# A hybrid encoder step on one core: a weight block's six matmuls become five, and each unit's two partial sums are added by ACT and DVE

## The chip, the cores and the metric

The kernel runs on one core of a Trainium2 chip. The metric is the time of one execution on the device in microseconds (us). Engine names are those of the profile: PE is TensorE's matmul (PEld its weight load), DVE is VectorE, ACT is ScalarE, POOL is GpSimd, SP is SyncE, whose queue (SPq) issues the DMAs.

## The reference

Two layers of an encoder step over 544 tokens (512 of a prompt, 32 of a second request) with 1024 features. Everything is float32.

```python
u = x @ w_in                      # 1024 -> 8192, split into qa ka va za qb kb vb zb xr zc ga gb gc
ya = band_attention(qa, ka, va, rel_table)          * silu(za)
yb = group_norm(retention(rope(qb), rope(kb), vb))  * silu(zb)
yc = rg_lru(conv(xr))                               * silu(zc)
m  = sigmoid(ga) * (ya @ w_branch[0]) + sigmoid(gb) * (yb @ w_branch[1]) + sigmoid(gc) * (yc @ w_branch[2])
r  = ALPHA * x + m @ w_out
r  = r + sigmoid(r @ w_ple_gate) * (p[l] @ w_ple)
x  = layer_norm(r)                # input of the next layer
```

The outputs are x after the second layer, and the caches and states of both layers.

## The kernel before

**Layout.** Activations lie with features on the 128 partitions and the N = 544 tokens along the free dimension. A float32 product is made of three products in the type fp32r: each operand is split into a high part (rounded to fp32r) and a low part (what is left), and high x high, high x low and low x high are summed in PSUM. `hilo` (L254) makes the two parts of an activation, a copy on ACT and a subtraction on DVE; `split` (L198) does the same for two blocks of weights at a time, 128x256 values.

**Blocks and units.** The weights come from memory in chunks of 8 blocks of 128x128 (tile `raw`, 512 KB, four buffers). A *unit* is 128 output features: a tile of PSUM named `mm` takes the sums of 2 blocks (kind `pl`, the per-layer embedding), 4 blocks (`bA`, `bB`, `bC`, the branch products) or 8 blocks (all others). `layer_units` (L33) lists the units of a layer in order: 8 `pl`; 4 `xr`, of which the first two form one group that fills both `mm` tiles block by block; `va`, `qa`/`ka` in turns, `kb`, `vb`, `qb`; then for each branch four `z` units and eight times a `g` unit and a `b` unit; then 8 `wo` and 8 `pg`.

`block` (L237) issues a block's six matmuls: for each of (weights high, x high), (weights high, x low), (weights low, x high), one for each half of the tokens, 272 columns each. A tile `mm` is two banks of PSUM of 512 float32; each half of the tokens has a bank of its own. There are two such tiles, so PE can fill one while the other is emptied by `evac` (L788): by ACT, by DVE or by both, according to the kind of the unit.

**Order.** The order of the work is written out by hand. Each engine executes its instructions in the order in which the program issues them. Before each block `tick` (L165) is called: it lets `stream` (L208) issue the splits up to `LEAD` = 8 blocks ahead, and it advances the *jobs*: generators for attention, retention, the recurrence (rg_lru) and the layer norm, which issue a few instructions and then sleep for the number of ticks that they yield (table `PACE`). So the side work is woven in between the blocks. Split weights lie in seven buffers of two blocks each (pool `wp`, tiles `wh` and `wl`), or in `held` tiles of a chunk where they are kept longer.

**Ends of a layer.** The last `pg` units (from the 7th in layer 0, from the 3rd in layer 1, `HELD`) and the first two `xr` units of layer 1 are computed by halves of the tokens (`by_halves`, L932): first all blocks of half 0, then those of half 1, so that the layer norm of half 0 (`ln_job`, L730) runs beside the matmuls of half 1. In layer 1's beginning the `pl` units run while the layer norm of layer 0 is under way. At the start of the kernel `x_job` (L994) makes the parts of the eight input tiles, one every two ticks from tick 5 on, beside the `pl` units of layer 0.

**Storage of the parts.** The high and low parts of x are in four slabs: two for the high parts (`xh`), two for the low ones (`xl`), four feature tiles each. The same holds for the gated branch outputs (`zah`, `zal` and so on), for m (`mh`, `ml`) and, in one slab, for the embedding (`phl`).

Of the kernel before, what the change touches and what calls it, by code (L numbers as in the profile page):

```python
# [19 lines left out]
H2 = N // 2  # L20
PAST = 256
# [96 lines left out]
def encoder(ctx: ExitStack, tc, xT, pT, W, RB, KC, VC, PAR, CST, o_y, o_k, o_v, o_rp, o_rs, o_cv, o_lr):  # L118
# [7 lines left out]
    wp = pool("wp", LEAD // 2 + 3)  # L126
# [71 lines left out]
    def split(n, h, lo):  # L198
        t = raw[n // 8][:, n % 8:n % 8 + 2]
        S.copy(h, t)  # L200
        V.tensor_tensor(lo, t, h.bitcast(F32), SUB)  # L201
        parts[n // 2] = (h, lo)

    def hold(n):
        held[n // 8] = sl("held", F32R, (128, 2, 8, 128))
        return [[held[n // 8][:, i, k:k + 2] for i in range(2)] for k in range(0, 8, 2)]

    def stream(lead=LEAD):  # L208
        while at["split"] < L * NB and at["split"] <= at["use"] + at["more"] + lead:
            n = at["split"]  # L210
            kind, f, k = BLOCKS[n % NB]
            if n // 2 not in parts:
                if kind == "wg" or kind == "pg" and f >= HELD[n // NB]:
                    if n % 8 == 0:
                        at["hold"] = hold(n)
                    h, lo = at["hold"][n % 8 // 2]
                else:
                    h = wp.tile([128, 2, 128], F32R, tag="wh", name="wh")
                    lo = wp.tile([128, 2, 128], F32R, tag="wl", name="wl")
                split(n, h, lo)  # L220
                if n % 8 == 6:
                    load()
            at["split"] += 2


    def split_ahead(l):
        for c in range((l + 1) * NCH, (l + 1) * NCH + (AT["xr"] + 16) // 8):
            t = wr.tile([128, 8, 128], F32, tag="raw", name="raw")
            raw[c] = t
            Q.dma_start(out=t, in_=W[c // NCH, c % NCH])  # L230
            views = hold(8 * c)
            yield 8
            for i, v in enumerate(views):
                split(8 * c + 2 * i, *v)
                yield 3

    def block(ps, xh, xl, first, last, hfs=(0, 1), n=None):  # L237
        if n is None:
            n = at["use"]
            at["use"] += 1  # L240
        h, lo = parts[n // 2]
        for i, (w, x) in enumerate(((h, xh), (h, xl), (lo, xh))):
            for hf in hfs:
                T.matmul(ps[:, hf, :H2], lhsT=w[:, n % 2, :], rhs=x[:, hf * H2:(hf + 1) * H2],  # L244
                         start=first and i == 0, stop=last and i == 2)

    def halves(ap):
        return ap.rearrange("p (a b) -> p a b", a=2)
# [10 lines left out]
    def busy(n):  # L259
        ps = psum("mm")  # L260
        for _ in range(n):
            T.matmul(ps[:, 0, :H2], lhsT=zero[:, :128], rhs=zero, start=True, stop=True)  # L262


    st = {"xh": [sl("xh", F32R) for _ in range(2)], "xl": [sl("xl", F32R) for _ in range(2)]}
# [3 lines left out]
    def ple_load(l):  # L269
        pr = sl("pr")  # L270
        ple_in[l] = (pr, sl("phl", F32R))
        for k in range(2):
            Q.dma_start(out=pr[:, k], in_=pT[l, :, k])

    def ple_split(l):
        pr, p2 = ple_in[l]
        for k in range(2):
            hilo(p2[:, k], p2[:, 2 + k], pr[:, k])
# [34 lines left out]
    def layer(l, env, nxt):  # L313
# [165 lines left out]
        def lru_tile(t):  # L479
# [12 lines left out]
            for g in range(2):  # L492
                w, lo = ([parts[(l * NB + AT["wg"] + g * 4 + t) // 2][i][:, t % 2] for i in range(2)])
# [206 lines left out]
        def span(hf):  # L700
            return slice(0, N) if hf is None else slice(hf * H2, (hf + 1) * H2)

# [6 lines left out]
        def ln_center():  # L709
            yield PACE["center"]  # L710
            c, s2 = tmp("center"), env["s2p"]
            for h in range(2):
                ps = psum("sc")
                T.matmul(ps[:, :H2], lhsT=cst[:, C_O1K:C_O1K + 128], rhs=env["acc"][:, span(h)])
                S.mul(c[:, span(h)], ps[:, :H2], 4.0)
# [11 lines left out]
        PIECES = [(c if i < 2 else H2 - 128, c, min(128, H2 - c), 0 if i < 2 else 128 - (H2 - c))  # L727
                  for i, c in enumerate((0, 128, 256))]

        def ln_job(hf):  # L730
            ones = cst[:, C_O1K:C_O1K + 1]
            if hf and l == L - 1:
                busy(WARM[1])
            ps = psum("tp")
            for q, src in enumerate((env["s1"], env["s2"])):
                for i, (c0, _, _, _) in enumerate(PIECES):
                    T.matmul(ps[:, 3 * q + i:3 * q + i + 1], lhsT=src[:, hf * H2 + c0:hf * H2 + c0 + 128], rhs=ones)
# [3 lines left out]
            mu, e2, sq, A, B = (w[:, 3 * i:3 * i + 3] for i in range(5))  # L741
            V.tensor_copy(w[:, 0:6], ps[:, 0:6])
            V.tensor_tensor(sq, mu, mu, MUL)
            V.scalar_tensor_tensor(sq, e2, EPS, sq, ADD, SUB)
            G.tensor_tensor(A, sq, mhalf, ALU.pow)
# [3 lines left out]
            for q, src in enumerate((B, A)):  # L749
                ps = psum("sc" if hf == 0 else "tp" if q == 0 else "pv")  # L750
                for i, (_, d0, n, i0) in enumerate(PIECES):
                    T.matmul(ps[:, d0:d0 + n], lhsT=bc(src[:, i:i + 1], [[0, 128]]), rhs=ident[:, i0:i0 + n])
                AB.append(ps[:, :H2])
# [9 lines left out]
            for f in range(9):  # L763
# [11 lines left out]
                if f and not last:  # L775
                    e = f - 1
                    h, lo = (st[k][e // 4][:, e % 4, span(hf)] for k in ("xh", "xl"))
# [10 lines left out]
        def evac(kind, t, ps, hf=None):  # L788
            pv = ps[:, :, :H2]
            if kind in KEY:  # L790
# [3 lines left out]
                d = halves(env[key][:, t])  # L794
# [4 lines left out]
                if kind == "ka":  # L799
# [3 lines left out]
                    V.tensor_copy(env["kn"][:, t], ps[:, 1, H2 - NS:H2])  # L803
# [13 lines left out]
            elif kind == "qa":  # L817
# [3 lines left out]
                h = halves(env["QTh"][:, t])  # L821
                S.mul(h, pv, 0.125)
                V.scalar_tensor_tensor(halves(env["QTl"][:, t]), pv, 0.125, h.bitcast(F32), MUL, SUB)
                S.mul(env["qs"][:, t], ps[:, 1, H2 - NS:H2], 0.125)
            elif kind == "xr":
# [5 lines left out]
                S.copy(xrp[:, t, 3:3 + H2], ps[:, 0, :H2])  # L831
                S.copy(xrp[:, t, 3 + H2:3 + NP], ps[:, 1, :NP - H2])
                S.copy(xrp[:, t, NP + 6:], ps[:, 1, NP - H2:H2])  # L833
# [4 lines left out]
            elif kind in ("za", "zb", "zc"):  # L838
# [15 lines left out]
            elif kind[0] == "g":
                sg = tmp("sg")
                S.activation(halves(sg), pv, AF.Sigmoid)  # L856
                env["sg", t] = sg
            elif kind[0] == "b":
                sg = env.pop(("sg", t))
                a, b = t // 4, t % 4  # L860
                if kind == "bC":
                    if b == 0:
                        env["m", a] = sl("m")
                    V.tensor_tensor(halves(env["m", a][:, b]), pv, halves(sg), MUL)
                else:
                    V.tensor_tensor(halves(sg), pv, halves(sg), MUL)  # L866
                    m = env["m", a][:, b]
                    (V if kind == "bB" and t == 7 else G).tensor_tensor(m, m, sg, ADD)  # L868
                    if kind == "bB":
                        if b == 0:  # L870
                            env["mh", a], env["ml", a] = sl("mh", F32R), sl("ml", F32R)
                        hilo(env["mh", a][:, b], env["ml", a][:, b], m)
            elif kind == "pl":
                if t % 4 == 0:
                    env["ple", t // 4] = sl("ple")
                S.copy(halves(env["ple", t // 4][:, t % 4]), pv)
            elif kind == "wo":
# [3 lines left out]
                r, xh_, xl_ = env["r", a][:, b], st["xh"][a][:, b], st["xl"][a][:, b]  # L881
                V.scalar_tensor_tensor(halves(r), halves(xh_.bitcast(F32)), ALPHA, pv, MUL, ADD)
# [10 lines left out]
        def gate(t, ps, hf):  # L893
            r = rt(t, hf)
            sg = tmp("sg")[:, span(hf)]
            if hf is None:
                S.activation(halves(sg), ps[:, :, :H2], AF.Sigmoid)
            else:
                S.activation(sg, ps[:, hf, :H2], AF.Sigmoid)  # L899
# [32 lines left out]
        def by_halves(units, together):  # L932
# [4 lines left out]
            for hf in range(2):  # L937
                for i, (u, k) in enumerate(order):
# [4 lines left out]
                    if not together and k == 0:  # L943
                        pss[u] = psum("mm")
                    block(pss[u], st["xh"][k // 4][:, k % 4], st["xl"][k // 4][:, k % 4], k == 0, k == 7, (hf,),
                          first + i if hf else None)
# [7 lines left out]
        for group in UNITS:  # L954
# [139 lines left out]
```

## Time and profile before

| What | us |
|---|---|
| median of 3 timed executions | 1337.95 |
| lowest and highest | 1337.41, 1338.74 |
| the profiled execution | 1333.96 |
| its span, from the first to the last instruction | 1332.2 |
| PE busy, of the span | 1307.9 |
| DVE busy | 778.8 |
| ACT busy | 596.6 |

The profile is that of one execution. Busy time is the union of an engine's instructions; because matmuls are pipelined, the busy time of PE also covers time in which it streams nothing, and the distance from one matmul's start to the next is the better measure of PE's speed. The mean granted clock of TensorE was 0.993 of full speed.

### The profile page before, as it was taken

Reading aid. Unit: us, or ns where it says so; the run is one execution under the profiler, and the core shown is the slowest. Engines: PE = TensorE matmul, PEld = TensorE weight load, DVE = VectorE, ACT = ScalarE, POOL = GpSimd, SP = SyncE. Lnnn points to the kernel's source line nnn. Section 1 sums busy time; section 2 is a strip of 40 time slices with the busy share of each in tenths; the row PEclk is TensorE's granted clock in tenths of the full one; section 3 lists DMA queues with packets and bytes.
Section 4 is the critical chain, followed back from the end, with each engine's and each line's share of the span. In section 5 each row is a group of like instructions: output and inputs, shape, how many; then the busy total and the mean of one; then the engine's idle time right before and its main releaser. Section 6 shows DMA issues by size and latency. Waiting matters only on the chain.

```text
span 1332.2 us, 26812 instructions
## 1 busy us (share of the span) xinstructions
PE 1307.9 (98%) x10783; PEld 1272.4 (96%) x10783; DVE 778.8 (58%) x1663; ACT 596.6 (45%) x1491; POOL 201.9 (15%) x192
## 2 busy tenths in 40 slices
PE   9999999999999999999999999999999999999985
PEld 9998899999999999999899998999999999999985
DVE  5666563673854444468884756547548545435587
ACT  6765544432642333334467654444245323333333
POOL 0210121320101101002312102133001110110034
PEclk9999999999999999999999999999999999999998
DMA  7233422221222222233112353232212222222201
GB/s 293 64 129 96 155 82 87 90 89 63 70 91 96 80 96 82 93 104 120 64 62 99 86 158 113 72 98 77 75 64 95 80 96 81 88 87 95 96 17 68
DMA packets 44285, 124.96 MB, mean 94 GB/s; under 512 B 9344, under 2 KB 13696, under 8 KB 43520
## 3 DMA queue, kind: packets, MB, share of 16 engines
q1 hardware_dynamic: 44160, 123.24, 28.3%
q8 instruction: 85, 1.39, 0.4%
q14 instruction: 40, 0.33, 0.1%
HBM read 111.52 MB, written 7.24 MB: 89 GB/s over the span
## 4 chain that ended last, share of the span: by engine, by line
PE 89%; DVE 6%; ACT 3%; issue 2%; POOL 0%; DVEq 0%; ACTq 0%; POOLq 0%
PE mm L244 78%; PE pv L413 2%; PE sc L386 1%; PE tp L402 1%; PE sc L639 1%; PE tp L322 1%; DVE held L201 1%; PE pv L653 1%; ACT wh L200 1%; PE mm L262 1%; DVE wl L201 1%; DVE r L718 1%; PE pv L657 1%; PE pv L497 0%; DVE s L923 0%
## 5 line engine op out<-in xcount | busy, mean ns | idle before, releaser
L201 DVE TENSOR_TENSOR wl<-raw,wh 128x256 fp32r<-128x256 f32 x704 | 306.6, 470 | 298.9 <-ACT wh L200 298.0
L244 PE MATMUL mm<-xh,wh 128*128 128x272 f32 x2144 | 455.4, 294 | 0.5 <-ACT xrp L833 0.5
L244 PE MATMUL mm<-xl,wh 128*128 128x272 f32 x2144 | 443.5, 288 | 0.0
L244 PE MATMUL mm<-xh,wl 128*128 128x272 f32 x2144 | 442.1, 287 | 0.4 <-DVE wl L201 0.4
L244 PEld LDWEIGHTS mm<-xh,wh 128*128 128x128 f32 x2144 | 334.3, 188 | 13.9 <-issue 9.9
L244 PEld LDWEIGHTS mm<-xh,wl 128*128 128x128 f32 x2144 | 335.9, 188 | 0.6 <-DVE wl L201 0.6
L244 PEld LDWEIGHTS mm<-xl,wh 128*128 128x128 f32 x2144 | 335.0, 188 | 0.0
L200 ACT CAST wh<-raw 128x256 fp32r<-128x256 f32 x704 | 251.0, 403 | 52.1 <-PE mm L244 49.3
L856 ACT ACTIVATE sg<-mm 128x544 f32<-128x544 f32 x48 | 30.0, 625 | 144.1 <-PE mm L244 144.1
L868 POOL TENSOR_TENSOR m<-m,sg 128x544 f32<-128x544 f32 x30 | 42.5, 1418 | 313.3 <-DVE sg L866 313.3
L244 PE MATMUL mm<-xh,held 128*128 128x272 f32 x320 | 64.8, 296 | 6.8 <-ACT sg L899 5.1
L347 ACT ACTIVATE sx<-sx,sst 128x128 f32<-128x128 f32 (+4 forms) x68 | 37.9, 558 | 66.7 <-DVE sst L345 63.9
L244 PEld LDWEIGHTS mm<-xh,held 128*128 128x128 f32 x320 | 51.6, 192 | 9.0 <-ACT sg L899 5.5
L244 PE MATMUL mm<-ml,wh 128*128 128x272 f32 x256 | 52.9, 288 | 0.0
L244 PE MATMUL mm<-mh,wl 128*128 128x272 f32 x256 | 52.8, 288 | 0.0
L244 PE MATMUL mm<-mh,wh 128*128 128x272 f32 x256 | 52.7, 287 | 0.0
L866 DVE TENSOR_TENSOR sg<-mm,sg 128x544 f32<-128x544 f32 x32 | 23.2, 725 | 41.3 <-PE mm L244 41.3
L255 ACT CAST xh<-r 128x544 fp32r<-128x544 f32 (+1 forms) x32 | 17.1, 533 | 66.6 <-DVE r L883 63.7
L244 PE MATMUL mm<-xl,held 128*128 128x272 f32 x160 | 46.6, 291 | 0.0
L244 PEld LDWEIGHTS mm<-mh,wl 128*128 128x128 f32 x256 | 40.1, 188 | 0.0
L244 PEld LDWEIGHTS mm<-mh,wh 128*128 128x128 f32 x256 | 40.1, 188 | 0.0
L244 PEld LDWEIGHTS mm<-ml,wh 128*128 128x128 f32 x256 | 40.0, 188 | 0.0
(257 smaller groups left out, 1855.1 us busy)
## 6 DMA issues: line engine op xcount, KB each, us to landing
raw<-in_W SPq DMA_DIRECT2D x189, 512.0 KB, 3.2
bias<-in_RB SPq DMA_DIRECT2D x16, 256.0 KB, 3.9
x<-in_xT SPq DMA_DIRECT2D x4, 544.0 KB, 8.9
o_v<-VA SPq DMA_DIRECT2D x2, 1088.0 KB, 5.6
o_k<-KT SPq DMA_DIRECT2D x2, 1088.0 KB, 5.2
swap<-KB SPq DMA_DIRECT2D x32, 68.0 KB, 2.8
swap<-QB SPq DMA_DIRECT2D x32, 68.0 KB, 2.0
o_y<-r SPq DMA_DIRECT2D x6, 272.0 KB, 2.2
```

The lines of the kernel that those rows point to most:

```text
L200: S.copy(h, t)
L201: V.tensor_tensor(lo, t, h.bitcast(F32), SUB)
L244: T.matmul(ps[:, hf, :H2], lhsT=w[:, n % 2, :], rhs=x[:, hf * H2:(hf + 1) * H2], start=first and i == 0, stop=last and i == 2)
L255: S.copy(h, src)
L262: T.matmul(ps[:, 0, :H2], lhsT=zero[:, :128], rhs=zero, start=True, stop=True)
L322: T.transpose(tp[:rows, t * 128:(t + 1) * 128], src[:, t, c0:c0 + rows], ident)
L347: S.activation(x, x, AF.Exp, bias=s[:, 0:1], scale=-1.0, accum_out=s[:, 1:2])
L386: T.matmul(scs[j][:, o:o + n], lhsT=q_[r, p, i * 128:i * 128 + 128], rhs=k_[r, p, :n], start=k == 0, stop=k == 2)
L413: T.matmul(pv[64 * j:64 * j + 64, i * 128:i * 128 + 128], lhsT=env["vatok"][:, kt, h * 64:h * 64 + 64], rhs=xs[j][:, o:o + 128], start=kt ...
L856: S.activation(halves(sg), pv, AF.Sigmoid)
L866: V.tensor_tensor(halves(sg), pv, halves(sg), MUL)
L868: (V if kind == "bB" and t == 7 else G).tensor_tensor(m, m, sg, ADD)
```

## The change

1. **Tokens are cut at 256 instead of 272.** `SPANS` are columns 0 to 255 and 256 to 543. The by-halves code and the layer norm use these spans; the layer norm's pieces of 128 columns are two for the first span and three for the second.
2. **Five matmuls a block.** The parts of an activation tile now lie side by side in one slab (`pairs`: shape 128 x 2 tiles x 2 parts x 544), so that one operand can take columns 0 to 255 of the high part and then those of the low part: 512 columns. The weights' high part times these is one matmul into the first bank: the sums with the high part in its columns 0 to 255, those with the low part in its columns 256 to 511. Columns 256 to 543 take three matmuls of 288 columns into the second bank, as before. The weights' low part times the first 256 high columns is added to bank columns 256 to 511.
3. **Merge.** Before a unit is emptied, `merge` copies the first 256 columns to a tile `hh` with ACT, and DVE adds them to the next 256 in place. From there on the 544 sums lie contiguously in PSUM, and `evac` reads them as one range (the copy of an `xr` unit takes two instructions instead of three).
4. **Weights are split in fours**, 128x512 values, except in the kernel's first chunk (twos). The pool `wp` has four buffers of four blocks. `load` is called when the second four of a chunk are issued, and `split_ahead` yields 6 ticks after each four instead of 3 after each two.

The core of the diff:

```diff
+HA = 256
+SPANS = ((0, HA), (HA, N))
+HIGH, MM0 = 0, HA
...
-    wp = pool("wp", LEAD // 2 + 3)
+    wp = pool("wp", LEAD // 4 + 2)
...
-            return ps_mm.tile([128, 2, 512], F32, tag="mm", name="mm")
+            return ps_mm.tile([128, 1024], F32, tag="mm", name="mm")
...
-    def split(n, h, lo):
-        t = raw[n // 8][:, n % 8:n % 8 + 2]
-        S.copy(h, t)
-        V.tensor_tensor(lo, t, h.bitcast(F32), SUB)
-        parts[n // 2] = (h, lo)
+    def split(n, h, lo, step=4):
+        for k in range(0, 4, step):
+            t = raw[n // 8][:, n % 8 + k:n % 8 + k + step]
+            S.copy(h[:, k:k + step], t)
+            V.tensor_tensor(lo[:, k:k + step], t, h[:, k:k + step].bitcast(F32), SUB)
+        parts[n // 4] = (h, lo)
...
-                    h = wp.tile([128, 2, 128], F32R, tag="wh", name="wh")
-                    lo = wp.tile([128, 2, 128], F32R, tag="wl", name="wl")
-                split(n, h, lo)
-                if n % 8 == 6:
+                    h = wp.tile([128, 4, 128], F32R, tag="wh", name="wh")
+                    lo = wp.tile([128, 4, 128], F32R, tag="wl", name="wl")
+                split(n, h, lo, 2 if n < 8 else 4)
+                if n % 8 == 4:
                     load()
-            at["split"] += 2
+            at["split"] += 4
...
-                split(8 * c + 2 * i, *v)
-                yield 3
+                split(8 * c + 4 * i, *v)
+                yield 6
...
-    def block(ps, xh, xl, first, last, hfs=(0, 1), n=None):
+    def block(ps, x, first, last, hfs=(0, 1), n=None):
...
-        h, lo = parts[n // 2]
-        for i, (w, x) in enumerate(((h, xh), (h, xl), (lo, xh))):
-            for hf in hfs:
-                T.matmul(ps[:, hf, :H2], lhsT=w[:, n % 2, :], rhs=x[:, hf * H2:(hf + 1) * H2],
-                         start=first and i == 0, stop=last and i == 2)
+        h, lo = (w[:, n % 4, :] for w in parts[n // 4])
+        pl = bass.AP(x.tensor, x.offset, [x.ap[0], [x.ap[1][0], 2], [1, HA]])
+        if 0 in hfs:
+            T.matmul(ps[:, :2 * HA].rearrange("p (a b) -> p a b", a=2), lhsT=h, rhs=pl, start=first, stop=False)
+        if 1 in hfs:
+            for i in range(2):
+                T.matmul(ps[:, 2 * HA:HA + N], lhsT=h, rhs=x[:, i, HA:], start=first and i == 0, stop=False)
+        if 0 in hfs:
+            T.matmul(ps[:, MM0:MM0 + HA], lhsT=lo, rhs=x[:, 0, :HA], start=False, stop=last)
+        if 1 in hfs:
+            T.matmul(ps[:, 2 * HA:HA + N], lhsT=lo, rhs=x[:, 0, HA:], start=False, stop=last)
+
+    def merge(ps):
+        t = sm.tile([128, HA], F32, tag="hh", name="hh", bufs=2)
+        S.copy(t, ps[:, HIGH:HIGH + HA])
+        V.tensor_tensor(ps[:, MM0:MM0 + HA], ps[:, MM0:MM0 + HA], t, ADD)
...
+    def pairs(name):
+        t = sl(name, F32R, (128, 2, 2, N))
+        return [t[:, 0], t[:, 1]]
+
+    st = [x for _ in range(4) for x in pairs("x")]
...
         def evac(kind, t, ps, hf=None):
-            pv = ps[:, :, :H2]
+            pv = ps[:, MM0:MM0 + N]
+            if hf != 1:
+                merge(ps)
```

More of the change, by code (lines that the diff above doesn't have):

```diff
@@ L196, in load @@
             at["load"] = c + 1
-    def split(n, h, lo):
-        t = raw[n // 8][:, n % 8:n % 8 + 2]
-        S.copy(h, t)
-        V.tensor_tensor(lo, t, h.bitcast(F32), SUB)
-        parts[n // 2] = (h, lo)
+    def split(n, h, lo, step=4):
[4 more added lines that the diff above has]
+        parts[n // 4] = (h, lo)
     def hold(n):
         held[n // 8] = sl("held", F32R, (128, 2, 8, 128))
-        return [[held[n // 8][:, i, k:k + 2] for i in range(2)] for k in range(0, 8, 2)]
+        return [[held[n // 8][:, i, k:k + 4] for i in range(2)] for k in range(0, 8, 4)]
     def stream(lead=LEAD):
@@ L211, in stream @@
             kind, f, k = BLOCKS[n % NB]
-            if n // 2 not in parts:
+            if n // 4 not in parts:
                 if kind == "wg" or kind == "pg" and f >= HELD[n // NB]:
@@ L261, in busy @@
         for _ in range(n):
-            T.matmul(ps[:, 0, :H2], lhsT=zero[:, :128], rhs=zero, start=True, stop=True)
-    st = {"xh": [sl("xh", F32R) for _ in range(2)], "xl": [sl("xl", F32R) for _ in range(2)]}
+            T.matmul(ps[:, :H2], lhsT=zero[:, :128], rhs=zero, start=True, stop=True)
+    def pairs(name):
+        t = sl(name, F32R, (128, 2, 2, N))
+        return [t[:, 0], t[:, 1]]
+    st = [x for _ in range(4) for x in pairs("x")]
     x0 = [sl("x0") for _ in range(2)]
@@ L270, in ple_load @@
         pr = sl("pr")
-        ple_in[l] = (pr, sl("phl", F32R))
+        ple_in[l] = (pr, pairs("phl"))
         for k in range(2):
@@ L492, in lru_tile @@
             for g in range(2):
-                w, lo = ([parts[(l * NB + AT["wg"] + g * 4 + t) // 2][i][:, t % 2] for i in range(2)])
+                w, lo = ([parts[(l * NB + AT["wg"] + g * 4 + t) // 4][i][:, t] for i in range(2)])
                 ps = psum("sc"), psum("pv")
@@ L700, in span @@
         def span(hf):
-            return slice(0, N) if hf is None else slice(hf * H2, (hf + 1) * H2)
+            return slice(0, N) if hf is None else slice(*SPANS[hf])
         def hfs_(hf):
@@ L713, in ln_center @@
                 ps = psum("sc")
-                T.matmul(ps[:, :H2], lhsT=cst[:, C_O1K:C_O1K + 128], rhs=env["acc"][:, span(h)])
-                S.mul(c[:, span(h)], ps[:, :H2], 4.0)
+                n = SPANS[h][1] - SPANS[h][0]
+                T.matmul(ps[:, :n], lhsT=cst[:, C_O1K:C_O1K + 128], rhs=env["acc"][:, span(h)])
+                S.mul(c[:, span(h)], ps[:, :n], 4.0)
             yield 2
@@ L725, in ln_center @@
             G.tensor_tensor(s2, s2, sq, ADD)
-        PIECES = [(c if i < 2 else H2 - 128, c, min(128, H2 - c), 0 if i < 2 else 128 - (H2 - c))
-                  for i, c in enumerate((0, 128, 256))]
+        PIECES = [[(c, c) for c in range(a, b - 127, 128)] + [(b - 128, b - (b - a) % 128)] * ((b - a) % 128 > 0)
+                  for a, b in SPANS]
         def ln_job(hf):
             ones = cst[:, C_O1K:C_O1K + 1]
+            np_ = len(PIECES[hf])
+            first = SPANS[hf][0]
             if hf and l == L - 1:
@@ L735, in ln_job @@
             for q, src in enumerate((env["s1"], env["s2"])):
-                for i, (c0, _, _, _) in enumerate(PIECES):
-                    T.matmul(ps[:, 3 * q + i:3 * q + i + 1], lhsT=src[:, hf * H2 + c0:hf * H2 + c0 + 128], rhs=ones)
+                for i, (c0, _) in enumerate(PIECES[hf]):
+                    T.matmul(ps[:, np_ * q + i:np_ * q + i + 1], lhsT=src[:, c0:c0 + 128], rhs=ones)
             if hf and l == L - 1:
@@ L750, in ln_job @@
                 ps = psum("sc" if hf == 0 else "tp" if q == 0 else "pv")
-                for i, (_, d0, n, i0) in enumerate(PIECES):
-                    T.matmul(ps[:, d0:d0 + n], lhsT=bc(src[:, i:i + 1], [[0, 128]]), rhs=ident[:, i0:i0 + n])
-                AB.append(ps[:, :H2])
+                for i, (c0, d0) in enumerate(PIECES[hf]):
+                    T.matmul(ps[:, d0 - first:c0 + 128 - first], lhsT=bc(src[:, i:i + 1], [[0, 128]]),
+                             rhs=ident[:, d0 - c0:128])
+                AB.append(ps[:, :SPANS[hf][1] - first])
             A = tmp("lnA")[:, span(hf)]
@@ L776, in ln_job @@
                     e = f - 1
-                    h, lo = (st[k][e // 4][:, e % 4, span(hf)] for k in ("xh", "xl"))
+                    h, lo = (st[e][:, i, span(hf)] for i in range(2))
                     hilo(h, lo, rt(e, hf))
@@ L793, in evac @@
                     env[key] = sl(key)
-                d = halves(env[key][:, t])
+                d = env[key][:, t]
                 if kind == "kb":
@@ L820, in evac @@
                     env["qs"], env["kn"] = (qs.tile([128, 4, NS], F32, name=k) for k in ("qs", "kn"))
-                h = halves(env["QTh"][:, t])
+                h = env["QTh"][:, t]
                 S.mul(h, pv, 0.125)
-                V.scalar_tensor_tensor(halves(env["QTl"][:, t]), pv, 0.125, h.bitcast(F32), MUL, SUB)
-                S.mul(env["qs"][:, t], ps[:, 1, H2 - NS:H2], 0.125)
+                V.scalar_tensor_tensor(env["QTl"][:, t], pv, 0.125, h.bitcast(F32), MUL, SUB)
+                S.mul(env["qs"][:, t], pv[:, NP:], 0.125)
             elif kind == "xr":
@@ L830, in evac @@
                 xrp = env["xrp"]
-                S.copy(xrp[:, t, 3:3 + H2], ps[:, 0, :H2])
-                S.copy(xrp[:, t, 3 + H2:3 + NP], ps[:, 1, :NP - H2])
-                S.copy(xrp[:, t, NP + 6:], ps[:, 1, NP - H2:H2])
+                S.copy(xrp[:, t, 3:3 + NP], pv[:, :NP])
+                S.copy(xrp[:, t, NP + 6:], pv[:, NP:])
                 if t == 3:
@@ L875, in evac @@
                     env["ple", t // 4] = sl("ple")
-                S.copy(halves(env["ple", t // 4][:, t % 4]), pv)
+                S.copy(env["ple", t // 4][:, t % 4], pv)
             elif kind == "wo":
@@ L895, in gate @@
             sg = tmp("sg")[:, span(hf)]
[L896 to L899, printed above, removed]
+            S.activation(sg, ps[:, MM0:MM0 + N][:, span(hf)], AF.Sigmoid)
             yield 1
@@ L944, in by_halves @@
                         pss[u] = psum("mm")
-                    block(pss[u], st["xh"][k // 4][:, k % 4], st["xl"][k // 4][:, k % 4], k == 0, k == 7, (hf,),
-                          first + i if hf else None)
+                    block(pss[u], st[k], k == 0, k == 7, (hf,), first + i if hf else None)
                     if not together and k == 7:
```

58 lines of the change are left out of this document (26 added, 32 removed).

## The prediction

> **What bounds the kernel now.** I read the page first: busy shares, then the chain that ended last.
>
> ```profile
> span 1332.2 us, 26812 instructions
> PE 1307.9 (98%) x10783; PEld 1272.4 (96%) x10783; DVE 778.8 (58%) x1663; ACT 596.6 (45%) x1491; POOL 201.9 (15%) x192
> ...
> PE 89%; DVE 6%; ACT 3%; issue 2%; POOL 0%; DVEq 0%; ACTq 0%; POOLq 0%
> ```
>
> PE carries 89% of the chain, DVE and ACT 9%. Busy PE says little, since matmuls overlap, so I took busy times by stage next, and the waits of PE.
>
> ```profile
> 5.00:20.00 15.00, 15.00 (x109) 14.46 (x109) 10.39 (x19) 12.83 (x29) 0.00 (x0) 1.00 0.93 360
> ...
> 653.00:690.00 37.00, 34.94 (x263) 34.06 (x263) 30.42 (x65) 24.94 (x62) 12.33 (x14) 0.95 0.09 29
> 1266.00:1312.00 46.00, 40.15 (x301) 38.86 (x300) 37.85 (x70) 18.20 (x49) 20.25 (x19) 0.96 0.11 37
> ```
> ```profile
> 466.00:533.00 67.00, 67.00 (x537) 67.00 (x536) 29.49 (x64) 24.21 (x61) 6.77 (x5) 1.00 0.27 88
> ```
> ```profile
> PE mm L244 <- ACT sg L899: 5.1, 2, 3.1
> PE tp L752 <- DVE lnst L746: 1.5, 1, 1.5
> ```
>
> Columns: window, then PE, PEld, DVE, ACT, POOL busy with counts, granted clock, DMA. In the merge branches (466 to 533 us) PE starts 537 matmuls of 272 columns in 67 us, **124.8 ns each**, with DVE at 44% and ACT at 36%: nothing but PE counts there. PE hardly ever waits: its longest entry is 5.1 us. But three stages are not so free: the first 15 us (ACT 86% busy), the change of layer (653 to 690: DVE 82%) and the end (1266 to 1312: DVE 82%, PE only 87%).
>
> **The change, part by part.**
>
> *One matmul less a block.* There are 752 blocks a layer, 1504 in all, at six matmuls each (9024). Before, a block streams 6 x 272 = 1632 columns; after, 512 + 3 x 288 + 256 = 1632. So the columns are the same, and the gain is one fixed cost f of a matmul per block, if PE's spacing is f plus a cost per column. The trace has other widths in the attention scores: pairs on 64 rows each, running side by side. From the QTl pair to the KTl pair both weight loads are long done. First and last step of 8 for each width:
>
> ```profile
> 95.19 0.28 PE L386 MATMUL sc<-KTh,QTl 64*128 64x256 f32 x2
> 95.31 0.28 PE L386 MATMUL sc<-KTl,QTh 64*128 64x256 f32 x2
> ...
> 112.24 0.39 PE L386 MATMUL sc<-KTh,QTl 64*128 64x512 f32 x2
> 112.47 0.39 PE L386 MATMUL sc<-KTl,QTh 64*128 64x512 f32 x2
> ```
> ```profile
> 832.88 0.28 PE L386 MATMUL sc<-KTh,QTl 64*128 64x256 f32 x2
> 833.00 0.28 PE L386 MATMUL sc<-KTl,QTh 64*128 64x256 f32 x2
> ```
> ```profile
> 850.35 0.39 PE L386 MATMUL sc<-KTh,QTl 64*128 64x512 f32 x2
> 850.57 0.39 PE L386 MATMUL sc<-KTl,QTh 64*128 64x512 f32 x2
> ```
>
> Unrounded, the eight steps at 256 columns take 115 to 122 ns (118.5 in the middle), those at 512 take 229 to 235 (231). The line through the two is 0.4395 ns a column and f = 6.0 ns; at 272 columns it gives 125.5, against the 124.8 seen on 128 rows, so I trust it. A block then costs 231 + 3 x 132.6 + 118.5 = 747, instead of 753 by the same line. **Gain: 6.0 x 1504 = 9 us.** Bounds: with 122 and 229 the line has f = 15 (22.6 us); with 115 and 235 it is below zero, which I cut at nothing, since no row shows a shorter instruction stream to cost more. That the 512 columns come in two runs of 256 from two planes is in no row; I take it as free, as every matmul's columns already come from an address of their own, and keep up to 4 ns a block (6 us) against it in the range.
>
> The Trainium skill, page "TensorE: Matmul & The Clock Gate", section "Back-to-back issue gap", gives columns/2.4 + 2.5 ns; that would be 115.8 ns at 272 columns, and the trace does not agree (124.8). By its 2.5 ns the gain would be 3.8 us and the sum below 5 us worse.
>
> *Split in fours instead of twos.* It costs less on ACT and DVE.
>
> ```profile
> L201 DVE TENSOR_TENSOR wl<-raw,wh 128x256 fp32r<-128x256 f32 x704 | 306.6, 470 | 298.9 <-ACT wh L200 298.0 <-PE mm L244 0.2
> L200 ACT CAST wh<-raw 128x256 fp32r<-128x256 f32 x704 | 251.0, 403 | 52.1 <-PE mm L244 49.3 <-DMA raw<-in_W 2.8
> ...
> L856 ACT ACTIVATE sg<-mm 128x544 f32<-128x544 f32 x48 | 30.0, 625 | 144.1 <-PE mm L244 144.1
> ...
> L403 ACT COPY sx<-tp 128x384 f32<-128x384 f32 x32 | 15.2, 476 | 4.7 <-PE tp L402 4.5
> ...
> L403 ACT COPY sx<-tp 128x512 f32<-128x512 f32 x16 | 9.4, 585 | 7.5 <-PE tp L402 7.5
> L876 ACT COPY ple<-mm 128x544 f32<-128x544 f32 x16 | 9.8, 613 | 4.2 <-PE mm L244 3.9
> ...
> L256 DVE TENSOR_TENSOR xl<-r,xh 128x544 fp32r<-128x544 f32 x16 | 11.6, 725 | 11.4 <-ACT xh L255 11.4
> ```
>
> DVE: 128x512 lies between 470 and 725, at some 695 ns; 378 instructions in place of about 756, so 263 us for the 334 of now. ACT: some 620 ns, 234 us for 271. Back-to-back pairs overlap today, so the queue gains less than these 71 and 37 us. None of it is on the path in the merge branches. The weight tiles hold 16 blocks instead of 14, and a chunk's load is issued two blocks earlier; at a DMA share of 0.27 SP's queue has room, and I count both as nothing.
>
> *The merge.* 112 units a layer, 224 in all: a 128x256 ACT copy out of PSUM (476 - (585 - 476) = 367 ns by the two L403 rows) and a 128x256 DVE addition (470). That is 82 us of ACT and 105 of DVE: with the fours both engines' totals rise by about 40. What matters is order. ACT and DVE take their queues in order (DVE idles 298 us for ACT in the L201 row, with later work behind it), so at each unit's end DVE waits for the copy, and ACT for the sum, wherever ACT also empties the tile. Emptying comes about 0.9 us later. With two PSUM tiles, a unit's emptying has the next unit's time: 6 us for eight blocks, 3 us for four, but 1.5 us for two (pl). So I go by stages.
>
> *First pl units.* Rows of one unit now:
>
> ```profile
> 11.62 0.41 ACT L200 CAST wh<-raw 128x256 fp32r<-128x256 f32 x1
> ...
> 11.93 0.65 ACT L255 CAST xh<-x 128x544 fp32r<-128x544 f32 x1
> ...
> 12.61 0.62 ACT L876 COPY ple<-mm 128x544 f32<-128x544 f32 x1
> 12.61 0.72 DVE L256 TENSOR_TENSOR xl<-x,xh 128x544 fp32r<-128x544 f32 x1
> ...
> 13.12 0.41 ACT L200 CAST wh<-raw 128x256 fp32r<-128x256 f32 x1
> ```
>
> ACT has no gap: wh, xh, ple, wh again after 1.50 us, PE's own pace. After: xh 0.65; the sum cannot start on DVE before xl is done (0.03 + 0.72), then 0.44; ple 0.54; half of a split in fours 0.26: 2.6 us a unit. Six units have an xh (it starts at tick 5 of 16): 6 x 1.1 = 6.6, less the 1.5 us by which the second tile lets PE run ahead: **+5 us.** Bounds: 0 (all hidden) and 9.
>
> By the Trainium skill, the same page's paragraph on engine queue depths, ACT and DVE are strict FIFO; were they not, this cost would shrink to the copy's 0.37 a unit, some 2 us. The 298 us of the L201 row agree with the page.
>
> *Change of layer.* Eight pl units again, as filling while the layer norm runs on DVE and ACT.
>
> ```profile
> 660.39 1.50 PE L737 MATMUL tp<-cst,s 128*128 128x1 f32 x12 [1.13 <-DVE s L920]
> ...
> 672.32 0.40 PE L244 MATMUL mm<-xh,held 128*128 128x272 f32 x1 [0.33 <-ACT ple L876]
> ```
> ```profile
> 681.36 0.43 DVE L256 TENSOR_TENSOR xl<-r,xh 128x272 fp32r<-128x272 f32 x1
> ```
> ```profile
> 683.32 0.29 PE L244 MATMUL mm<-xh,held 128*128 128x272 f32 x1
> ...
> 684.69 0.52 PE L244 MATMUL mm<-xh,wh 128*128 128x272 f32 x2 [0.46 <-ACT xrp L833]
> ```
>
> Eight sums put 8 x 0.47 = 3.8 us on DVE (82% busy) and 8 x 0.37 = 3 on ACT. The last x half is ready at 681.8 and first used at 683.3, so 1.5 us of the 6.8 is cover, and part runs side by side: **+4 us**, between 1 and 7. The xr pair, which holds both tiles, makes PE wait for ACT already; the merge adds 0.37 + 0.44, less 0.1 for one copy saved: 0.7 a layer, **+1.4 us.**
>
> *Attention, gates, end.* Transposes have already waited for DVE once; elsewhere there is room:
>
> ```profile
> 102.28 0.90 PE L402 MATMUL tp<-cst,sx 128*128 128x128 f32 x3 [0.48 <-DVE sx L352]
> ```
> ```profile
> 778.46 0.59 ACT L403 COPY sx<-tp 128x512 f32<-128x512 f32 x1 [0.65 <-PE tp L402]
> ...
> 780.61 1.09 PE L413 MATMUL pv<-sx,vatok 128*64 128x128 f32 x16
> ```
>
> The copy ends at 779.05 and its matmul is at 780.61, 1.5 us against 0.9 us of delay: I take **+2 us** for the 24 steps, between 0 and 10 (0.4 each). A gate unit is followed by one of only 3 us; 0.37 + 0.47 + 0.63 plus a queue of up to 0.7 + 1.0 just passes it now and then: **+1 us.** At the end DVE gains six sums (2.8) and saves 1.2 on splits, and the second half, the one that ends last, has 288 columns for 272 (48 blocks x 3 x 16 x 0.44 ns = 1.0 us more on PE, while the shorter first half lies where PE waits anyway). The first half's norm takes two pieces instead of three. Part of the 1.6 us on DVE is covered: **+2 us.**
>
> Sum: -9 + 5 + 4 + 1.4 + 2 + 1 + 2 = **+6 us.** The profiled execution took 1333.96 us (span 1332.2), 4 us below the median 1337.95; the same +6 there gives 1340, on the median **1344**.
>
> **The rivals.**
>
> 1. *The fixed cost is larger.* Should f be 15 ns (the upper line), the gain is 22.6 us, and with all 15.4 us of waits the kernel ends at 1331. It turns on one number, in each block: above 10.2 ns (15.4 / 1504) the change pays, above 12 visibly. For it: 128 rows are not 64. Against: 124.8 lies on the line.
> 2. *The second tile hides the merges.* Waits shrink to some 4 us: 1337.95 - 9 + 4 = 1333. For it: PE's waits are few now. Against: ACT's gapless first units.
> 3. *The change doesn't do what it says:* columns alone set the time, f = 0, or the two runs eat it: 1353. For it: 272 columns at 124.8 and 512 at 231 are 0.459 and 0.451 ns a column, nearly alike.
> 4. *Both halves meet:* gain 9, waits 9: 1338.
>
> **How the numbers follow.** Forecast 0.38 (slower 0.33, within 0.2% 0.05); rival 1: 0.18, faster; rival 2: 0.17 (faster 0.14, same 0.03); rival 3: 0.17, slower; rival 4: 0.10 (same 0.08, faster 0.02). Together: faster 0.34, same 0.16, slower 0.50, with 0.2% (2.7 us) as about what a measurement of this kernel can tell from no change. The forecast alone spans 1338 to 1350. The range goes from 1327 (rival 1's gain with 11.7 us of waits) to 1357 (rival 3 with 4 us more of attention waits).
>
> **What would show it.** Spacing in the merge branches: 747 ns a block (f = 6), 738 (f = 15), 753 (f = 0), read as matmuls per stretch: five per block. The pl units at the start 2.6 us apart instead of 1.5, with ACT idle for the sum; the first xr matmul some 5 us later. 128x512 splits at 695 and 620 ns, about 378 each; 224 copies at 367 and additions at 470. Between 653 and 690 a stretch longer by 4. The forecast is wrong if pl units stay at 1.5 us, or if attention transposes begin to wait for DVE in most steps.

## The result, and the profile after

The changed kernel took a median of **1404.26 us** (1401.88 to 1406.07, four runs) against 1337.72 us for the kernel before on the same chip (four runs): a ratio of **1.0495, 95% interval 1.0473 to 1.0517**, 66 us slower. The forecast was 1344 us with a range from 1327 to 1357. The direction was right, the size was not.

The first two parts of the changed kernel's page and its chain of what ended last:

```profile
span 1404.3 us, 23192 instructions
...
PE 1329.7 (95%) x9263; PEld 1213.4 (86%) x9263; DVE 828.8 (59%) x1509; ACT 635.6 (45%) x1329; POOL 213.4 (15%) x192
...
PE 67%; DVE 17%; ACT 10%; issue 4%; DMA 1%; SPq 0%; POOL 0%; ACTq 0%; DVEq 0%; POOLq 0%
```

PE's share of the chain fell from 89% to 67%; DVE and ACT now hold 27%, not 9%. Their busy shares hardly moved (58 to 59%, 45 to 45%). So it looks less like how much DVE and ACT do than when they do it; the experiments below test that.

Did the matmuls get slower? Busy time in one stretch of the merge branches of the changed kernel:

```profile
466.00:533.00 67.00, 67.00 (x447) 62.95 (x447) 35.92 (x53) 25.29 (x50) 7.91 (x5) 1.00 0.28 87
```

447 matmuls in 67 us are 149.9 ns each, 749 ns for a block of five. Before, 537 in 67 us were 124.8 ns, 749 ns for a block of six. **A block costs the same: five instructions or six, 1632 columns.** The gain that was to pay for everything does not show.

The waits of PE, summed by whom it waited for (us in total, times, longest):

```profile
PE mm L251 <- ACT ple L900: 13.4, 11, 2.4
PE mm L251 <- ACT sg L880: 10.1, 7, 2.6
PE mm L251 <- ACT sg L920: 9.4, 4, 5.2
PE tp L342 <- ACT vatok L343: 3.2, 2, 1.6
```

PE waits for tiles to be emptied (`ple`, `sg`), where before its longest entry was 5.1 us. To see where, I took, in the order of issue, the time from a stage's first block to the next stage's first block in both profiled executions. us before, then what four kernels take in addition (e3, e5 and e2 come below):

| Stage | before | changed | e3 | e5 | e2 |
|---|---|---|---|---|---|
| layer 0: pl | 13.3 | +6.8 | +7.0 | +5.4 | +0.5 |
| xr | 25.4 | +6.7 | +3.9 | +1.9 | -0.1 |
| va to qb (attention, side work) | 197.5 | +8.6 | +12.5 | +7.0 | -1.2 |
| zc, gC, bC (retention beside) | 116.7 | +9.8 | +10.0 | +5.1 | 0.0 |
| the branches A and B | 192.7 | +0.2 | +0.3 | +0.8 | +0.2 |
| wo, pg | 102.7 | +7.9 | +6.1 | +4.2 | +3.5 |
| layer 1: pl | 18.1 | +7.0 | +6.9 | +5.2 | +1.5 |
| xr | 26.2 | +5.3 | +5.1 | +3.6 | -0.1 |
| va to qb | 197.5 | +6.8 | +12.5 | +6.0 | -1.2 |
| zc, gC, bC | 116.8 | +9.2 | +9.9 | +5.1 | 0.0 |
| the branches A and B | 192.3 | +0.6 | +0.8 | +0.8 | +0.3 |
| wo, pg, to the end | 128.2 | +2.3 | +8.7 | +3.7 | -0.5 |

The sum is 71.2 us, and 0.9 us more pass before the first block: the 72.1 by which the spans differ. Where DVE has little side work (branches A and B, 385 us of the kernel) hardly anything is lost (0.8 us). The rest is lost where DVE has side work, at the start and at the ends of the layers. Not all of it is the merge's: in layer 0, `wo` and `pg` lose 3.5 us in e2 too, which has no merge.

One loss in full: the gate unit gC0 of layer 0, in the timeline of the changed kernel (start, length; the bracket is the engine's idle time and who ended it).

```profile
297.73 2.98 DVE L206 TENSOR_TENSOR wl<-raw,wh 128x512 fp32r<-128x512 f32 x2
297.95 0.36 ACT L262 COPY hh<-mm 128x256 f32<-128x256 f32 x1
...
299.32 0.39 PE L256 MATMUL mm<-zc,wl 128*128 128x256 f32 x1 [0.96 <-DVE wl L206]
...
300.64 0.41 DVE L621 TENSOR_TENSOR kv<-kv,cst 128x256 f32<-128x256 f32 x1
...
301.08 0.43 DVE L620 TENSOR_TENSOR kv<-kv 128x256 f32<-128x256 f32 x1
301.54 0.42 DVE L621 TENSOR_TENSOR kv<-kv,cst 128x256 f32<-128x256 f32 x1
301.89 0.43 DVE L263 TENSOR_TENSOR mm<-mm,hh 128x256 f32<-128x256 f32 x1
302.35 0.62 ACT L880 ACTIVATE sg<-mm 128x544 f32<-128x544 f32 x1 [4.03 <-DVE mm L263]
```
```profile
303.02 0.50 PE L251 MATMUL mm<-x,wh 128*128 128x512 f32 x1 [0.94 <-ACT sg L880]
```

The copy is done at 298.31. The addition, 0.43 us of work, starts at 301.89: DVE first does what was issued before it, two splits (3 us, beside a POOL addition) and retention's decay chain (`kv`). ACT idles 4 us for it, and PE waits 0.94 us for the tile, after 0.96 us for the low part of the weights that came out of the first of these splits. The same unit before:

```profile
272.91 2.78 DVE L201 TENSOR_TENSOR wl<-raw,wh 128x256 fp32r<-128x256 f32 x3
...
274.75 0.62 ACT L856 ACTIVATE sg<-mm 128x544 f32<-128x544 f32 x1 [1.33 <-PE mm L244]
...
275.61 0.41 DVE L601 TENSOR_TENSOR kv<-kv,cst 128x256 f32<-128x256 f32 x1
```

DVE was behind there too, and it hurt no one: ACT alone emptied the tile, as soon as PE was done.

In the table of groups the same shows as a change of the releaser (busy, mean ns, then idle time before it and who ended it):

```profile
L206 DVE TENSOR_TENSOR wl<-raw,wh 128x512 fp32r<-128x512 f32 x350 | 263.4, 768 | 156.7 <-ACT wh L205 156.6
L205 ACT CAST wh<-raw 128x512 fp32r<-128x512 f32 x350 | 208.1, 618 | 3.2 <-PE mm L254 2.7 <-DMA raw<-in_W 0.6
L263 DVE TENSOR_TENSOR mm<-mm,hh 128x256 f32<-128x256 f32 x224 | 96.2, 429 | 205.9 <-ACT hh L262 205.5
L262 ACT COPY hh<-mm 128x256 f32<-128x256 f32 x224 | 83.3, 372 | 313.6 <-PE mm L258 312.4 <-PE mm L256 1.1
L880 ACT ACTIVATE sg<-mm 128x544 f32<-128x544 f32 x48 | 30.0, 625 | 37.8 <-DVE mm L263 37.8
```

The 48 sigmoids of the gates were released by PE before (the L856 row of the prediction); now all of their waiting is for DVE.

### The profile page after: what moved, and what is told of

Same layout as the page of the kernel before. It is cut to its first block, busy times and chain, and to the rows that moved or that the text cites. A ratio compares the mean times of both kernels' runs of the same rounds, so it can differ in the third digit from the quotient of the medians.

```text
span 1404.3 us, 23192 instructions
## 1 busy us (share of the span) xinstructions
PE 1329.7 (95%) x9263; PEld 1213.4 (86%) x9263; DVE 828.8 (59%) x1509; ACT 635.6 (45%) x1329; POOL 213.4 (15%) x192
## 4 chain that ended last, share of the span: by engine, by line
PE 67%; DVE 17%; ACT 10%; issue 4%; DMA 1%; SPq 0%; POOL 0%; ACTq 0%; DVEq 0%; POOLq 0%
PE mm L254 21%; PE mm L251 19%; PE mm L258 10%; PE mm L256 9%; DVE wl L206 3%; DVE mm L263 2%; ACT wh L205 2%; PE pv L433 1%; PE tp L422 1%; DMA raw<-in_W 1%; PE sc L406 1%; DVE r L739 1%; DVE sq L710 1%; DVE xc L507 1%; DVE r L923 1%
## 5 line engine op out<-in xcount | busy, mean ns | idle before, releaser
L251 PE MATMUL mm<-x,wh 128*128 128x512 f32 x1072 | 442.3, 413 | 19.9 <-ACT sg L880 10.1
L254 PE MATMUL mm<-x,wh 128*128 128x288 f32 x2144 | 460.0, 296 | 0.0
L254 PEld LDWEIGHTS mm<-x,wh 128*128 128x128 f32 x2144 | 406.5, 190 | 50.3
L206 DVE TENSOR_TENSOR wl<-raw,wh 128x512 fp32r<-128x512 f32 (+1 forms) x354 | 265.0, 764 | 160.9 <-ACT wh L205 160.7
L258 PE MATMUL mm<-x,wl 128*128 128x288 f32 x1072 | 319.1, 298 | 0.0
L256 PE MATMUL mm<-x,wl 128*128 128x256 f32 x1072 | 303.4, 283 | 0.9 <-DVE wl L206 0.9
L251 PEld LDWEIGHTS mm<-x,wh 128*128 128x128 f32 x1072 | 203.2, 190 | 35.3 <-ACT sg L880 11.5
L262 ACT COPY hh<-mm 128x256 f32<-128x256 f32 x224 | 83.3, 372 | 313.6 <-PE mm L258 312.4
L263 DVE TENSOR_TENSOR mm<-mm,hh 128x256 f32<-128x256 f32 x224 | 96.2, 429 | 205.9 <-ACT hh L262 205.5
L205 ACT CAST wh<-raw 128x512 fp32r<-128x512 f32 (+1 forms) x354 | 209.5, 615 | 6.2 <-DMA raw<-in_W 3.6
L256 PEld LDWEIGHTS mm<-x,wl 128*128 128x128 f32 x1072 | 202.9, 189 | 1.6 <-DVE wl L206 1.6
L258 PEld LDWEIGHTS mm<-x,wl 128*128 128x128 f32 x1072 | 202.5, 189 | 0.0
```

Source lines behind the costliest of these rows:

```text
L205: S.copy(h[:, k:k + step], t)
L206: V.tensor_tensor(lo[:, k:k + step], t, h[:, k:k + step].bitcast(F32), SUB)
L251: T.matmul(ps[:, :2 * HA].rearrange("p (a b) -> p a b", a=2), lhsT=h, rhs=pl, start=first, stop=False)
L254: T.matmul(ps[:, 2 * HA:HA + N], lhsT=h, rhs=x[:, i, HA:], start=first and i == 0, stop=False)
L256: T.matmul(ps[:, MM0:MM0 + HA], lhsT=lo, rhs=x[:, 0, :HA], start=False, stop=last)
L258: T.matmul(ps[:, 2 * HA:HA + N], lhsT=lo, rhs=x[:, 0, HA:], start=False, stop=last)
```

## The experiments

Theory W: the merge's addition puts DVE, in its order, between PE and every emptying; that is the loss. Rivals: the coarser split (S), the five-matmul stream or the paired storage (M). The first four runs take them apart.

**e1: the split in fours alone.**

```diff
 # the kernel before, with:
+    wp = pool("wp", LEAD // 4 + 2)
+    def split(n, h, lo, step=4):
...
     # six matmuls of 272 columns, no merge
```

> The kernel before (six matmuls of 272 columns, no merge) with the weights split in fours and the four buffers of four blocks. Theory W (the loss of 66 us is the merge: its addition stands in DVE's queue behind side work, and no unit's tile is emptied before DVE comes to it): 1330 to 1345 us, since no merge is there. Rival S (the coarser split delays the queues or the weights): 1365 us or more.

Measured: 1338.39 us, ratio 1.001 (1.0001 to 1.002). S falls. Within it, the pg stage of layer 0 takes 4.1 us more and the two stages from va to qb take 1.1 and 1.2 us less.

**e2: the change without its merge.**

```diff
         def evac(kind, t, ps, hf=None):
             pv = ps[:, MM0:MM0 + N]
-            if hf != 1:
-                merge(ps)
```

> The changed kernel without the merge (the product of the weights' high part with the low parts of the first 256 columns' tokens alone is read there, the high product is left out); five matmuls, fours and the paired storage stay. Theory W: 1330 to 1348 us, and 749 to 752 ns a block, as the columns are the same. Rival M (the five-matmul stream or the paired storage is itself slower): stays near 1400. Rival S: 1365 or more.

Measured: 1336.64 us, ratio 0.9997 (0.9986 to 1.0007). M falls. With five matmuls a block and no merge the time is that of before, not below it. Busy time in the same stretch of e2:

```profile
466.00:533.00 67.00, 67.00 (x446) 62.90 (x445) 27.72 (x41) 22.16 (x39) 6.79 (x5) 1.00 0.29 87
```

**e3: the merge on the kernel before.** Zeros are added, so the sums are unchanged.

```diff
+    def merge(ps):
+        t = sm.tile([128, 256], F32, tag="hh", name="hh", bufs=2)
+        S.mul(t, ps[:, 0, :256], 0.0)
+        V.tensor_tensor(ps[:, 0, :256], ps[:, 0, :256], t, ADD)
...
             pv = ps[:, :, :H2]
+            if hf != 1:
+                merge(ps)
```

> The kernel before, six matmuls and split in twos, with a merge that changes nothing: ACT writes zero times 256 columns of the unit to a tile, DVE adds these to the same columns in PSUM, before the unit is emptied. Theory W: 1385 to 1425 us, the loss of the change without its other parts. Rivals M and S: 1335 to 1350.

Measured: 1418.34 us, ratio 1.0605 (1.0584 to 1.0626). The loss is there without any other part of the change, and, by the table of stages, mostly in the same places (the attention stages and the last one lose more). Two groups of e3:

```profile
L250 DVE TENSOR_TENSOR mm<-mm,hh 128x256 f32<-128x256 f32 x224 | 95.8, 428 | 178.7 <-ACT hh L249 178.6
...
L863 ACT ACTIVATE sg<-mm 128x544 f32<-128x544 f32 x48 | 30.0, 625 | 35.3 <-DVE mm L250 35.3
```

**e4: the copy without the addition.**

```diff
         S.copy(t, ps[:, HIGH:HIGH + HA])
-        V.tensor_tensor(ps[:, MM0:MM0 + HA], ps[:, MM0:MM0 + HA], t, ADD)
```

> The changed kernel with the copy of the merge alone; the addition is left out, so the high product of the first 256 columns is missing from the sums. Theory W, with DVE's place in the emptying as the cause: 1340 to 1360 us (224 copies of 0.37 us on ACT, which waits for nothing but PE). If the extra work or the order on ACT were the cause: 1385 or more.

Measured: 1342.42 us, ratio 1.0037 (1.0021 to 1.0052). 224 copies on ACT in every emptying cost 5 us; the addition makes up the rest.

The next question was whether the addition costs by its length (W2) or by its place (W1).

**e5: one column instead of 256, and no copy.**

```diff
+    def merge(ps):
+        V.tensor_tensor(ps[:, 0, :1], ps[:, 0, :1], zero[:, :1].bitcast(F32), ADD)
```

> The kernel before with a DVE addition of zeros to one single column of every unit's tile before it is emptied; no ACT copy. 224 additions of one column are some 20 to 35 us of DVE time against the 96 of the merge. Theory W1 (the order costs: the emptying now waits until DVE's queue reaches it): 1375 to 1415 us. Rival W2 (the work costs: 96 us more on DVE): 1338 to 1355.

Measured: 1381.59 us, ratio 1.0338 (1.0313 to 1.0363): 44 us. Two groups of e5:

```profile
L248 DVE TENSOR_TENSOR mm<-mm,zero 128x1 f32<-128x1 f32 x224 | 36.4, 163 | 192.2 <-PE mm L244 192.0
...
L861 ACT ACTIVATE sg<-mm 128x544 f32<-128x544 f32 x48 | 30.0, 625 | 164.3 <-DVE mm L248 164.3
```

An addition of 0.16 us (36 us in all, somewhat above what was expected) costs 44. **Over half of e3's 81 us comes with an addition of little more than a third of the merge's DVE time (36 of 96 us): the place costs.**

**e11: 256 columns, but no copy.**

```diff
+        V.tensor_tensor(ps[:, 0, :256], ps[:, 0, :256], zero[:, :256].bitcast(F32), ADD)
```

> The kernel before with a DVE addition of zeros to 256 columns of every unit's tile, without ACT's copy (e5 adds one column: 44 us; e3 copies and adds 256: 81 us). If the length of DVE's addition makes the difference of 37 us: 1400 to 1415. If it is ACT's copy ahead of the addition, the second hop: 1382 to 1395.

Measured: 1406.53 us, ratio 1.0507 (1.0476 to 1.0537; two runs). Against the kernel before on the same chip that is 67 us. So the place, with the shortest addition, costs 44, the addition's length some 23 more, the copy ahead of it the remaining 14 of e3; by the intervals, each of the two differences is uncertain by some 5 us.

**e6 and e7: the toll of e3 on a part of the units.** In e6 the 64 units that DVE empties anyway, in e7 the other 160.

```diff
-            if hf != 1:
+            if hf != 1 and (kind[0] == "b" or kind == "wo"):          # e6; e7 has "not (...)"
                 merge(ps)
```

> The toll of e3 (zero times 256 columns copied by ACT, added by DVE) on the 64 units alone whose tile DVE empties anyway (bA, bB, bC, wo). Theory W1: 1335 to 1348 us, as their emptying has always waited for DVE. Rival W2: 64 of 224 units, by share 80 x 64/224 = 23 us, so 1355 to 1365.

> The toll of e3 on the other 160 units, whose tile ACT empties first or alone. Theory W1: 1405 to 1420 us, nearly all of the 80 us of e3. Rival W2: by share 80 x 160/224 = 57 us, so 1385 to 1400.

Measured: e6 1337.72 us, ratio 1.0 (0.9986 to 1.0014); e7 1410.27 us, ratio 1.0552 (1.053 to 1.0575). The 64 merges cost nothing, the 160 cost 73 us. The gates' group in e6, then the addition in e6:

```profile
L863 ACT ACTIVATE sg<-mm 128x544 f32<-128x544 f32 x48 | 30.0, 626 | 128.7 <-PE mm L244 128.6
L250 DVE TENSOR_TENSOR mm<-mm,hh 128x256 f32<-128x256 f32 x64 | 27.5, 429 | 83.6 <-ACT hh L249 83.6
```

In e6 the gates are released by PE again, as before the change. Most of e6's 64 units lie in stages that lose hardly anything in e3 either (A, B, `wo`). The fair comparison is branch C, where DVE has side work: by stages as in the table, e6's eight merges a layer (the `bC` units) add 0.3 us there, e7's twelve (`zc` and `gC`) 8.5.

**e8: the 512 columns in one run.** The kernel of e2, with columns 0 to 511 of the high part in place of the two parts.

```diff
-        pl = bass.AP(x.tensor, x.offset, [x.ap[0], [x.ap[1][0], 2], [1, HA]])
+        pl = bass.AP(x.tensor, x.offset, [x.ap[0], [HA, 2], [1, HA]])
```

> The kernel of e2 with the 512 columns of the first matmul taken in one run (columns 0 to 511 of the high part) instead of 256 of the high and 256 of the low part; the sums are then others than the reference's. If two runs cost the 4 ns by which 512 columns take longer here (235) than on 64 rows (231): 6 us less than e2, 1328 to 1333 us. If not: 1334 to 1339 and 235 ns again, and the cost is by columns alone.

Measured: 1337.58 us, ratio 1.0001 (0.9989 to 1.0013), and in the same stretch:

```profile
466.00:533.00 67.00, 67.00 (x448) 62.96 (x448) 28.45 (x42) 21.60 (x39) 7.49 (x6) 1.00 0.29 92
```

448 against 446: two runs cost next to nothing (some 3 ns a block by these counts, nothing by the times), so the columns are what is paid for.

**e9: PE's gaps at the start filled.** After each block of the pl units 2 to 7 of layer 0, three matmuls of zeros into an unused tile.

```diff
                     block(ps, x, k == 0, k == nk - 1)
+                    if l == 0 and kind == "pl" and t > 1:
+                        fill = psum("tp")
+                        for _ in range(3):
+                            T.matmul(fill[:, :H2], lhsT=zero[:, :128], rhs=zero, start=True, stop=True)
```

> The changed kernel with three matmuls of zeros (272 columns, into the tile tp, which nothing uses then) behind each block of the pl units 2 to 7 of layer 0: they fill the 1.1 us by which PE waits in each of these units, and nothing else. Theory C (a part of the loss is TensorE's clock, granted at 0.5 from 27.6 to 34.4 us because PE stood idle in the pl units): the clock stays at 1.0 there, the first xr pair takes 12.5 to 13.5 us instead of 17.5, and the whole 1397 to 1402. Rival (the xr pair is slow because its splits and x parts come late): 17 us again, and 1404 to 1408.

The stretch of the first xr pair, in the changed kernel and in e9 (the last but two columns: the granted clock):

```profile
26.00:44.00 18.00, 15.64 (x82) 14.17 (x83) 8.11 (x24) 7.34 (x17) 0.00 (x0) 0.81 0.51 188
```
```profile
26.00:44.00 18.00, 15.77 (x102) 14.37 (x102) 9.84 (x28) 9.60 (x22) 0.00 (x0) 1.00 0.48 183
```

The clock, 0.81 in the mean there in the changed kernel, stays at 1.00, and the pair takes 14.8 instead of 17.5 us: 2.7 us of the loss at this place is the clock. The 12.5 to 13.5 that were expected are missed; before the change the pair took 12.5, and 1.3 us of what is left is PE's wait for the second tile within the pair, in e9 as in the changed kernel. That the filling kept the clock up is not shown: in e3 PE pauses for 0.8 us in each of these units, unfilled, and its granted clock from 26 to 44 us is 1.00 too (its pair takes 15.1 us). The whole is at 1402.52 us (ratio 1.0467 to 1.0505), which overlaps the changed kernel's interval: of the total nothing is shown.

**e10: a try for a version below both.** Fours, but twos for wo, pg and the next layer's first chunks.

```diff
-                split(n, h, lo, 2 if n < 8 else 4)
+                split(n, h, lo, 2 if n < 8 or kind in ("wo", "pg") else 4)
...
-                split(8 * c + 4 * i, *v)
+                split(8 * c + 4 * i, *v, 2)
```

> The kernel of e1 (six matmuls, no merge, split in fours) with splits in twos where wo and pg units and the next layer's first chunks are split. In e1 the pg stage of layer 0 took 4.1 us longer than before and the qa stages 1.2 us less each. If it is the coarser split at the end of the layer that cost the 4.1: 1333 to 1337 us, 0.1 to 0.3% below the kernel before. If these differ by chance alone: 1336 to 1340.

Measured: 1336.96 us, ratio 0.9997 (0.9987 to 1.0006): no gain, and the pg stage of layer 0 still took 5.0 us more than before. The longer instruction isn't its cause; four blocks are still split at a time. e10's trace shows where the time goes: ACT idles 6.92 us for the load of a chunk of the next layer, which was issued at 627.13 us (before: 615.62), its split stands in ACT's order ahead of the sigmoid (L898) that empties the tile, and PE idles 3.80 us until that is done. The same wait of ACT is in e1 and e2 (8.12 and 8.53 us). Why the load is issued later with the fours was not tried. None of the variants beats the kernel before.

## Why the prediction was wrong

*The gain* ("6.0 x 1504 = 9 us"): mis-sized, the runs show next to none. f = 6 came from a line through pairs of 64-row matmuls at two widths, and 125.5 against 124.8 at 272 columns seemed to confirm it. But that point lies between the two others and says little about where the line starts. Rival 3 had the better reading: the cost per column was nearly the same at 272 and at 512 (0.459 and 0.451 ns). e2 shows it: five matmuls, no merge, 1336.64 us, and in the branches A and B, where PE alone counts, its 512 blocks took 0.5 us more than before, where 6 ns a block would have saved 3.1. The 2.5 ns a matmul that the Trainium skill gives (page "TensorE: Matmul & The Clock Gate", section "Back-to-back issue gap") would have brought an estimated 3.8 us. Against e1, which has the same splits and six matmuls, e2 is 1.7 us shorter, uncertain by about 2 us: a gain of 9 us is excluded, one of a microsecond or two is not.

*The merge's own costs* were right: 372 ns for the copy (367 foreseen), 429 for the addition (470), 224 of each; splits 350 + 28 times at 618 ns on ACT (620) and some 768 on DVE (695: 687 in the mean where POOL was idle, 1110 for the 71 that overlapped POOL's work). And e1 shows that the fours are neutral in the sum.

*The waits* ("emptying comes about 0.9 us later", 15.4 us in all) are the step that failed; the stages lost 71 in the profiled executions, by far the most of it in waits for the merge: e4, which lacks only the addition, takes 62 us less. (Of the rest, 3.9 are a wait for a load and 2.7 the clock, both below; what the lower clock at the change of layer adds was not tried.) I added the merge's own time to the emptying and a little for the queue, and did not ask how far DVE is behind at each place. In the timeline above it was 3.6 us behind (298.31 to 301.89). ACT had emptied such tiles without DVE's queue, and e6 and e7 show that this is the point: 64 merges in units that DVE alone empties cost 0, 160 in those that ACT empties, first or alone, cost 73 us.

By stage, with the working of the prediction:
- *First pl units* (+5): 6.8. The mechanism was right, as this timeline of the changed kernel shows:

```profile
20.81 0.65 ACT L270 CAST x<-x 128x544 fp32r<-128x544 f32 x1
20.96 0.50 PE L251 MATMUL mm<-phl,wh 128*128 128x512 f32 x1 [1.10 <-ACT ple L900]
...
21.36 0.38 ACT L262 COPY hh<-mm 128x256 f32<-128x256 f32 x1
21.49 0.73 DVE L271 TENSOR_TENSOR x<-x,x 128x544 fp32r<-128x544 f32 x1 [1.23 <-ACT x L270]
...
22.13 0.43 DVE L263 TENSOR_TENSOR mm<-mm,hh 128x256 f32<-128x256 f32 x1
...
22.59 0.61 ACT L900 COPY ple<-mm 128x544 f32<-128x544 f32 x1 [0.86 <-DVE mm L263]
```

  x part, copy, DVE's turn, ple: the units were 2.3 and 2.9 us apart in turn, 2.6 in the mean, as worked out. The sum was low because the second tile's 1.5 us were taken as cover once for all.
- *xr* (0.7 a layer): 6.7 and 5.3. Missed in layer 0: the pair needs both tiles empty at once, and the clock fell (2.7 us, by e9). In layer 1 the granted clock is lower too, 0.89 in this stage against 1.00 before; the parts of the loss were not tried one by one.
- *Change of layer* (+4, with the xr pair): pg and wo 7.9, pl 7.0. Mis-sized; DVE was 82% busy there before, which was in the quoted rows and should have been read as a sign of a long queue. And 3.9 us of the 7.9 are one wait of PE behind a load, as in e10, which the merge only lengthens. These rows of the changed kernel show it:

```profile
666.44 0.62 ACT L205 CAST held<-raw 128x512 fp32r<-128x512 f32 x1 [7.18 <-DMA raw<-in_W]
...
668.92 0.62 ACT L920 ACTIVATE sg<-mm 128x544 f32<-128x544 f32 x1
...
669.60 0.80 PE L251 MATMUL mm<-x,wh 128*128 128x512 f32 x1 [3.87 <-ACT sg L920]
```

  The working counted the earlier loads "as nothing". In the pl units that follow, the granted clock is lower as well (last but two columns, changed kernel and before):

```profile
694.20:719.30 25.10, 19.80 (x107) 17.83 (x105) 17.59 (x39) 13.51 (x34) 10.29 (x13) 0.80 0.00 1
```
```profile
653.00:671.50 18.50, 17.22 (x126) 16.78 (x126) 15.59 (x32) 12.28 (x28) 9.22 (x11) 0.91 0.01 1
```

- *Attention and side work* (+2): 8.6 and 6.8, above the bound of 10 together; which waits make it up was not taken apart.
- *Gates* (+1): 19.0 in branch C (its z units among them), where retention runs beside it; in A and B 0.8. The 3 us between a gate and the next use of its tile were held against a queue of at most 1.7 us; in the timeline above it was 3.6.
- *End* (+2): 2.3. Its terms were not measured one by one, and e3 loses 8.7 in this stage, so that the number came out may be luck.

The sign was right for the reason given, but an upper bound of 10 us for attention and a range to 1357 came from bounding durations, not backlogs.

## What to carry to other kernels

Before an instruction is put into the emptying of a tile, look up how far behind its engine is at each stage, and not only how long the instruction takes or how busy the engine is on average: here 0.16 us of DVE work per unit cost 44 us, and a whole merge was free where DVE alone emptied the tile. Where matmuls follow each other without a gap, count columns; fewer and longer instructions with the same columns gained nothing here. And a change of one stage's waits can be tested backwards: put the suspected toll on the old kernel (e3) and see the loss come back, stage by stage.

## What the hardware showed that I had not expected

The granted clock fell after short gaps. In the pl units of the changed kernel PE paused for 1.1 us at most at a time, with matmuls between, and in the stretch that followed, with one more pause of 1.29 us, the granted clock was 0.81 in the mean; with the gaps filled (e9) it was 1.00. But such gaps do not always lower it: in e3, with pauses of 0.8 us in each of these units and one of 1.57 us in the pair, it was 1.00 too. The Trainium skill (page "TensorE: Matmul & The Clock Gate", section "What's actually happening") has that the clock is set by how busy PE has been, in a window of about 3.4 us. No single pause here came near that length; how busy is busy enough, these runs do not show.
